# Attention of a two-layer diffusion backbone: the order of four engines written down as a pipeline over three items, and results that share a bank with context scores

## The chip, the core and the metric

The kernel runs on one core of a Trainium2 chip. A core has five engines, each with its own stream of instructions: TensorE (PE in the profile; its weight loads stand apart as PEld), VectorE (DVE), ScalarE (ACT), GpSimd (POOL) and SyncE (SP), which issues transfers. An engine works through its stream in order and waits at an instruction until the semaphores of what it needs have come. Matrix products go to PSUM, eight banks of 512 fp32 values in each of 128 partitions. The metric is the device time of one execution in microseconds, as the median of several runs. Before the change it is 2926.64 us, the median of three (2921.7 to 2929.64).

## What is computed

Two layers over 1024 latent tokens (a grid of 16 rows and 64 columns) and 256 context tokens, width 1024. Layer 0 mixes by Fourier and Hyena groups, layer 1 by neighbourhood attention with 16 heads of 64, and each layer ends with a SwiGLU block. The change concerns the attention of layer 1 only:

```python
s_loc = jnp.einsum("bcqhd,bicjhd->bhcqij", q_r, k_b).astype(jnp.float32) * scale + bias[None]
s_loc = jnp.where(col_ok[:, :, None, :], s_loc, -jnp.inf)
s_ctx = jnp.einsum("bcqhd,bjhd->bhcqj", q_r, kc).astype(jnp.float32) * scale
s = jnp.concatenate([s_loc.reshape(...), s_ctx], axis=-1)
p = jax.nn.softmax(s, axis=-1).astype(v.dtype)
o = (einsum("bhcqij,bicjhd->bcqhd", p_loc, v_b) + einsum("bhcqj,bjhd->bcqhd", p_ctx, vc))
```

Every latent query sees a window of 8 rows by 16 columns, with a bias for the relative position, and all 256 context keys. `y_lat` is the result times `w_out`. Inputs and outputs are float32.

## The kernel before, in words

The program is written with a tile framework. It names tiles in pools (`tile_pool`, with a number of buffers), and the framework finds the dependencies, sets the semaphores and, from a simulated timeline, chooses the order of each engine's instructions. What is traced earlier has the better claim, but an instruction may be moved ahead of another. `issue_after` (`follow`) and `add_manual_dep` add edges by hand.

Precision comes from split operands: a factor is kept as a high and a low half (fp16, or fp32r for queries and keys), and a product is three matmuls (high by high, high by low, low by high).

The attention is cut into 64 *items*. A pair `pr` of heads (0 to 7) has two halves `hf` of the rows, and each half four column chunks `c`. An item holds 128 queries of two heads; for each head it needs 384 local keys (12 rows by 32 columns) and 256 context keys.

- `attn_prep` (L1895) is a generator that projects keys, context keys and queries of one pair, 40 groups of three matmuls into the two `pq` banks, and evacuates each product with ScalarE (high) and VectorE (low): L1951 to L1955 and L1964 to L1966. Between them `value` (L1916) loads a block of values (five per pair) and at once converts it to halves (L1933, L1934). The weights come through `halves_of` on SyncE's queue.
- `attn_item` (L2006) is a generator in three stages. First two bias loads on GpSimd's queue (L2012, tiles of pool `pg`, four buffers) and twelve score matmuls (L2023), context and local for two heads, into four `ps` banks, chained by `follow`. Then the softmax: VectorE takes the minimum over the context (L2033; signs are turned) and adds bias and minimum over the local scores (L2034), ScalarE takes the exponentials (L2036 context, L2038 local). The probabilities are turned by TensorE (L2055: 3 transposes a head, copied to halves at L2058 and L2059). The context part of the first 52 items is split by ScalarE and GpSimd (L2046, L2047) and turned by a DMA on SyncE's queue (L2048); that of the last 12 is turned by TensorE as a third block. Last 30 small matmuls with the values (L2076 to L2078) into one more `ps` bank, and VectorE's reciprocal and multiply (L2080, L2081). The `banks` edges (L2039) hold the next item's scores behind this item's reads.
- `attn_out` (L2087) runs once in four items: four transposes, two copies, a store to memory through GpSimd's queue.
- `attention` (L1980) prepares pair 0 and then goes over the items; between the stages it advances the next pair's preparation to a share of the way, 24 parts for a pair and eight items. After pair 7 a *filler* takes its place, `first_part(0)` (L2344): 6 of 8 blocks of the output projection for the first half of the rows, with weights loaded on GpSimd's queue (L2348), the sum added by VectorE (`add_h`, L2334). Its first column block counts each load of attention output as work. What is left of it runs after the items, then `last_part` (L2368).

PSUM is two pools for the whole program: `pp` with six banks (tiles `ps`) and `pq` with two. During the attention `PS()` goes round the six (L1983). The pools `p4`, `p2`, `pg`, `pt` and `pk` in SBUF hold 20, 34, 4, 6 and 4 tiles.

## Time and profile before

| | |
|---|---|
| median of three runs | 2926.64 us (2921.7 to 2929.64) |
| the profiled execution | 2919.06 us |
| its span, first to last instruction | 2917.3 us |
| granted TensorE clock, mean | 0.979 |
| busy: PE, DVE, ACT, POOL | 2766.0, 2066.4, 1621.9, 609.2 us |
| waits on GpSimd's queue for the transposes that free a bias tile, 1800 to 2235 us | 95.5 us in 57 |

The profile is one execution, recorded by the hardware, in microseconds from the span's start. A line of the timeline gives start, duration, engine, source line, operation, what is written and read, a count, and in brackets the idle time of the engine before it and what ended that. A line of groups gives count, busy time, mean in ns of one, then idle time before the group and its releasers. A line of waits reads: engine and line, what it waited for, total, times, longest. Many matmuls carry L283, the line of the helper, so they are told apart by tiles: `ps<-s,s` with 64 rows are scores, with 128 rows and 65 columns values; `pq<-s,wh` are projections. L274 is the helper for GpSimd's transfers, L268 that for SyncE's.

### The profile page before, as it was taken

Reading aid. Unit: us, or ns where it says so; the run is one execution under the profiler, and the core shown is the slowest. Engines: PE = TensorE matmul, PEld = TensorE weight load, DVE = VectorE, ACT = ScalarE, POOL = GpSimd, SP = SyncE. Lnnn points to the kernel's source line nnn. Section 1 sums busy time; section 2 is a strip of 40 time slices with the busy share of each in tenths; the row PEclk is TensorE's granted clock in tenths of the full one; section 3 lists DMA queues with packets and bytes.
Section 4 is the critical chain, followed back from the end, with each engine's and each line's share of the span. In section 5 each row is a group of like instructions: output and inputs, shape, how many; then the busy total and the mean of one; then the engine's idle time right before and its main releaser. Section 6 shows DMA issues by size and latency. Waiting matters only on the chain. (4 is left out here: it accounts for less than half of the span.)

```text
span 2917.3 us, 46351 instructions
## 1 busy us (share of the span) xinstructions
PE 2766.0 (95%) x16419; PEld 1693.1 (58%) x16419; DVE 2066.4 (71%) x3857; ACT 1621.9 (56%) x2859; POOL 609.2 (21%) x993
## 2 busy tenths in 40 slices
PE   6989999899989999999999999999989999999998
PEld 3755557888879644444555844666665444444555
DVE  5778777585457898877886766666666688765755
ACT  4674325454665676654564555656654476654543
POOL 1012013354121121212120012333333022112000
PEclk8999999999999999999999999999999999999999
DMA  7574435358695665656994897666665666424753
GB/s 264 185 272 170 153 114 173 110 171 303 249 355 176 204 222 190 208 198 254 329 325 152 295 334 270 156 150 160 156 173 186 218 248 224 156 98 176 243 195 116
DMA packets 322083, 607.60 MB, mean 208 GB/s; under 512 B 89910, under 2 KB 129528, under 8 KB 321850
## 3 DMA queue, kind: packets, MB, share of 16 engines
q1 hardware_dynamic: 252378, 384.38, 40.8%
q0 software_dynamic: 67168, 216.06, 20.4%
q10 hardware_dynamic: 2304, 4.20, 0.4%
q8 instruction: 129, 2.11, 0.3%
q14 instruction: 104, 0.85, 0.1%
HBM read 455.33 MB, written 135.53 MB: 203 GB/s over the span
## 5 line engine op out<-in xcount | busy, mean ns | idle before, releaser
L1449 PE MATMUL ps<-s,s 128*128 128x512 f16 x2064 | 467.2, 381 | 10.9 <-ACT g L1454 5.2
L1449 PEld LDWEIGHTS <-s 128*128 128x128 f16 x2640 | 258.0, 98 | 326.0 <-issue 17.8
L283 PE MATMUL ps<-s,wh 128*128 128x256 f32 (+3 forms) x1752 | 398.4, 331 | 11.2 <-ACT wh L287 5.4
L1218 ACT ACTIVATE s<-s,c 128x512 f16<-128x512 f32 (+1 forms) x324 | 232.7, 752 | 134.5 <-DMA s<-d 75.2
L1666 PE MATMUL ps<-s 128*128 128x512 f16 (+2 forms) x1308 | 303.4, 378 | 2.0 <-DVE s L1219 2.0
L1219 DVE SCALAR_TENSOR_TENSOR s<-s,c,s 128x512 f16<-128x512 f32 (+1 forms) x324 | 247.2, 793 | 77.2 <-ACT s L1218 76.2
L283 PE MATMUL pq<-s,wh 128*128 128x512 f16 (+1 forms) x1000 | 276.5, 354 | 9.5 <-DMA wh<-d 2.6
L283 PE MATMUL ps<-s,wl 128*128 128x256 f32 (+3 forms) x876 | 261.9, 331 | 1.1 <-DVE wl L289 0.9
L283 PEld LDWEIGHTS <-wh 128*128 128x128 f16 x1664 | 161.5, 99 | 172.1 <-issue 21.9
L1666 PEld LDWEIGHTS <-s 128*128 128x128 f16 x1536 | 148.5, 98 | 178.9 <-issue 7.0
L274 POOL DMA_DIRECT2D d<-s x201 | 109.1, 543 | 638.7 <-DVE s L1219 160.2
L283 PE MATMUL ps<-s,s 128*128 128x65 f16 (+5 forms) x2922 | 204.8, 244 | 29.0 <-ACT t L2036 14.1
L1449 PE MATMUL ps<-s,wh 128*128 128x512 f16 x616 | 185.8, 380 | 4.9 <-ACT wh L1218 3.4
L335 ACT CAST mat<-cs 128x1024 fp32r<-128x1024 f16 (+2 forms) x120 | 111.4, 934 | 140.1 <-PE ps L283 57.3
L283 PEld LDWEIGHTS ps<-s,wh 128*128 128x128 f32 x1088 | 178.2, 193 | 18.2 <-ACT wh L287 5.7
L283 PE MATMUL ps<-s,mat 128*128 128x512 f32 x696 | 180.5, 405 | 4.7 <-DVE s L289 4.3
L283 PE MATMUL pq<-s,wl 128*128 128x512 f16 (+1 forms) x500 | 173.7, 353 | 0.0
L283 PEld LDWEIGHTS <-s 128*128 128x128 f16 x2400 | 114.5, 98 | 73.9 <-issue 14.9
L283 PEld LDWEIGHTS ps<-s,mat 128*128 128x128 f32 x696 | 133.3, 194 | 38.8 <-DVE s L289 5.6
L1251 ACT ACTIVATE t<-s 128x1024 bf16<-128x1024 f32 (+1 forms) x164 | 141.6, 864 | 15.0 <-DVE c L470 8.6
L1449 PE MATMUL pq<-s,s 128*128 128x512 f16 x576 | 132.6, 380 | 0.7 <-ACT s L1218 0.6
L283 PEld LDWEIGHTS <-wl 128*128 128x128 f16 x832 | 82.0, 99 | 77.9 <-issue 2.6
(434 smaller groups left out, 5476.3 us busy)
## 6 DMA issues: line engine op xcount, KB each, us to landing
s<-d SPq DMA_DIRECT2D x294, 256.0 KB, 4.3
d<-s POOLq DMA_DIRECT2D x157, 256.0 KB, 3.6
s<-in_down SPq DMA_DIRECT2D x154, 256.0 KB, 4.9
s<-in_ada_w POOLq DMA_DIRECT2D x48, 512.0 KB, 5.1
g<-in_bias POOLq DMA_DIRECT2D x128, 192.0 KB, 3.1
s<-in_gate SPq DMA_DIRECT2D x46, 512.0 KB, 3.8
s<-in_up SPq DMA_DIRECT2D x46, 512.0 KB, 4.0
d<-g POOLq DMA_DIRECT2D x87, 256.0 KB, 3.2
```

Of the source, the lines that this page charges most:

```text
L274: self.last_ldr = self.nc.gpsimd.dma_start(out, in_).ins
L283: return self.nc.tensor.matmul(o, l, r, start=st, stop=sp).ins
L335: self.nc.scalar.copy(m, st)
L1218: nc.scalar.activation(hi, src, AF.Copy, scale=scale)
L1219: nc.vector.scalar_tensor_tensor(lo, src, scale, hi, op0=MUL, op1=SUB)
L1251: self.nc.scalar.activation(junk[:, :t.shape[1]], t, AF.Abs, scale=2.0 ** -15, accum_out=st[:, k:k + 1])
L1449: nc.tensor.matmul(ps, x[:, sl], y, start=first and j == 0 and x is wh and y is xh, stop=j == 3 and x is wl, skip_group_check=True)
L1666: m = nc.tensor.matmul(acc[j][:, c0:c1], x[:, sl], y[:, xs], start=first and k == 0, stop=last and k == 2, skip_group_check=True)
```

## The change

The four stages are no longer generators whose order is left to the scheduler. Inside `attention` the order of TensorE, ScalarE, VectorE and GpSimd is taken as written (`manual_schedule`); SyncE's stays with the scheduler. Step `k` of the loop works on three items: bias loads of item k+3, the output of item k-2 if it closes a half, the third turn of item k-1 if it has one, scores and softmax of item k+1, a third of the preparation, the turning transposes of item k, a third, the values of item k-1, the copies of item k's transposes, a third.

PSUM is divided anew for the attention (`accumulators`): two banks `pq` for projections, four `sc` for scores, two `tr` for transposes; the old pools are closed before and opened again after. The result of item k-1 has no bank of its own: it goes to the upper half of the bank that holds the first head's context scores of item k+1. The second head's bias moves from pool `pg` to pool `p2`. A block of values is loaded 11 or so projection groups before it is converted (`loads` and `turns`), and the weights of queries and of the next keys are loaded a little earlier. The hand-made edges go. The matmuls, transposes, exponentials and conversions, their shapes and numbers stay the same. The core of the diff:

```diff
@@ Builder.__init__
-        self.pp = ent(tc.tile_pool(name="pp", bufs=6, space=bass.MemoryType.PSUM))
-        self.pq = ent(tc.tile_pool(name="pq", bufs=2, space=bass.MemoryType.PSUM))
+        self.psum = ent(ExitStack())
+        self.accumulators(pp=6, pq=2)
...
+    def accumulators(self, **banks):
+
+        self.psum.close()
+        for name, n in banks.items():
+            pool = self.tc.tile_pool(name=name, bufs=n, space=bass.MemoryType.PSUM)
+            setattr(self, name, self.psum.enter_context(pool))
...
+    def SC(self):
+        return self.sc.tile([P, 512], F32, tag="sc", name=self.nm("sc"))
+    def TR(self):
+        return self.tr.tile([P, 512], F32, tag="tr", name=self.nm("tr"))
@@ attn_prep
+        qs, vt, staged = {}, [], {}
+        loads, turns = (1, 5, 10, 16, 22), (12, 16, 22, 28, 33)
+        step = 0
+
+        def lin(wh, wl, pc, view=lambda x: x):
+            nonlocal step, acc
+            yield None
+            acc = self.SC() if pr == 0 else self.PQ()
             for kb in range(KB):
                 for w, part in ((wh, 0), (wh, 1), (wl, 0)):
-                    self.mm(acc[pc][:, :WID[pc]], w[:, kb * P:(kb + 1) * P], view(u.ap(part, kb, pc)),
+                    self.mm(acc[:, :WID[pc]], w[:, kb * P:(kb + 1) * P], view(u.ap(part, kb, pc)),
                             kb == 0 and w is wh and part == 0, kb == KB - 1 and w is wl)
+                step += 1
+                for c in range(5):
+                    if step == loads[c]:
+                        load(c)
+                    if step == turns[c]:
+                        value(c)
                 yield WID[pc] / 1024
 
...
+        def load(c):
+            st = staged[c] = self.T()
             if c < 4:
...
+        def value(c):
+            st = staged.pop(c)
+            w = 512 if c < 4 else 256
...
+        acc = None
+        wk = self.halves_of("wk", 0) if pr == 0 else self.aw
         for pc in (0, 1, 2):
...
+            if pc == 1:
+                wq = self.halves_of("wq", pr)
+            yield from lin(*wk, pc)
...
+            if pc == 1 and pr < 7:
+                self.aw = self.halves_of("wk", pr + 1)
+            yield from lin(*wq, pc, by_chunk)
@@ attention
     def attention(self, u, fill):
-        self.prep = {}
+        self.prep, self.osb, self.aw = {}, {}, None
         self.od = [[self.DR([P, LAT], F16) for _ in range(2)] for _ in range(8)]
-        self.banks = 6
-        n = sum(self.attn_prep(0, u))
+        self.accumulators(pq=2, sc=4, tr=2)
+        n = sum(x or 0 for x in self.attn_prep(0, u))
         prep = (x for pr in range(1, 9) for x in (self.attn_prep(pr, u) if pr < 8 else fill))
-        load = (x for pr in range(8) for x in self.attn_load(pr))
-        items, done, self.scores = [], 0, []
-        ahead = 1
-        for k in range(64 + ahead):
-            it = next(load, None)
-            if it is not None:
-                items.append(it)
-            for stage in range(3):
-                i = k - ahead - stage
-                if 0 <= i < 64:
-                    next(items[i], None)
-                while done < (k * 3 + stage + 5) * n / 24:
-                    done += next(prep)
-        for it in items[-2:]:
-            for _ in it:
-                pass
-        self.banks = 8
+        items = [(pr, hf, c) for pr in range(8) for hf in (0, 1) for c in range(4)]
+        state = [{} for _ in items]
+        done = 0
+
+        def piece(step, k):
+            if 0 <= k < 64:
+                step(state[k], *items[k])
+
+        def fetch(target):
+            nonlocal done
+            while done < target:
+                done += next(prep) or 0
+
+        for k in range(2):
+            piece(self.attn_bias, k)
+        e = mybir.EngineType
+        with self.tc.manual_schedule(engines={e.PE, e.Activation, e.DVE, e.Pool}):
+            for k in range(-1, 65):
+                piece(self.attn_bias, k + 3)
+                piece(self.attn_send, k - 2)
+                piece(self.attn_late, k - 1)
+                piece(self.attn_scores, k + 1)
+                fetch((k * 3 + 8) * n / 24)
+                piece(self.attn_turn, k)
+                fetch((k * 3 + 9) * n / 24)
+                free = state[k + 1]["free"] if k + 1 < 64 else self.SC()[:, 256:]
+                if 0 <= k - 1 < 64:
+                    self.attn_values(state[k - 1], *items[k - 1], free)
+                piece(self.attn_turned, k)
+                fetch((k * 3 + 10) * n / 24)
+            piece(self.attn_send, 63)
         for _ in prep:
+        self.accumulators(pp=6, pq=2)
+
+    def attn_bias(self, s, pr, hf, c):
...
+        for hd in (0, 1):
+            b = (self.S2 if hd else self.G)(F32, 384)
+            self.ldr(b, self.a["bias"][pr * 2 + hd, hf, c])
...
+    def attn_scores(self, s, pr, hf, c):
...
+        loc, pctx = ([self.SC(), self.SC()] for _ in range(2))
...
-                    with self.follow(last):
-                        last = self.mm(acc[hd][:, :w], qc[x][r], keys[y][r], x == 0 and y == 0, x == 1)
-                    first = first or last
+                    self.mm(acc[hd][:, :w], qc[x][r], keys[y][r], x == 0 and y == 0, x == 1)
...
-        for r in reads if self.scores[-1] is not own else ():
-            self.tc.add_manual_dep(self.scores[-1], r.ins.name, mybir.DependencyInfo(
-                mybir.DependencyClass.Sync, mybir.DependencyReason.DATA), reason="banks")
...
+        s["pts"], s["free"] = [None] * 3, pctx[0][:, 256:]
+        s["ways"] = [(1, bias[0], 3), (2, bias[1], 3)]
...
+            s["ways"].insert(1, (0, pc, 4))
+
+    def attn_turn(self, s, *item):
+
+        s["ps"] = []
+        for k, src, n in s["ways"][:2]:
+            ps = self.TR()
             for j in range(n):
-                nc.tensor.transpose(ps[:, j * P:(j + 1) * P], src[:, j * P:(j + 1) * P], self.ident)
+                self.nc.tensor.transpose(ps[:, j * P:(j + 1) * P], src[:, j * P:(j + 1) * P], self.ident)
+            s["ps"].append((k, ps, n * P))
+        del s["ways"][:2]
+
+    def attn_turned(self, s, *item):
+
+        for k, ps, w in s["ps"]:
+            t = s["pts"][k] = self.S2(F16, 1024)
+            self.nc.scalar.copy(t[:, :w], ps[:, :w])
+            self.nc.vector.tensor_tensor(t[:, 512:512 + w], ps[:, :w], t[:, :w], SUB)
+
+    def attn_late(self, s, *item):
+
+        if s["ways"]:
+            self.attn_turn(s)
+            self.attn_turned(s)
+
+    def attn_values(self, s, pr, hf, c, o):
...
-        if c == 3:
-            self.attn_out(pr, hf, osb[hf])
-        yield
...
+    def attn_send(self, s, pr, hf, c):
+
+        if c < 3:
+            return
...
+        ps = self.TR()
@@ run, first_part
+                if pc == 0:
+                    yield None
```

In a step, `attn_scores` writes the twelve matmuls and then, for each head in turn, the minimum, the bias step and the two exponentials, so that the reads of one bank follow one another; `attn_values` writes the 30 matmuls, the reciprocal and the multiply.

More of the change, by code (lines that the diff above doesn't have):

```diff
@@ L1936, in value @@
             vt.append((v, lo))
-        if pr == 0:
-            self.aw = self.halves_of("wk", 0)
-        acc = {}
-        wk = self.aw
+        acc = None
+        wk = self.halves_of("wk", 0) if pr == 0 else self.aw
         for pc in (0, 1, 2):
-            for i, s in enumerate(lin(*wk, pc, acc)):
-                if i == 3:
-                    value(len(vt))
-                if pc == 1 and i == 6:
-                    wq = self.halves_of("wq", pr)
-                yield s
+            if pc == 1:
+                wq = self.halves_of("wq", pr)
+            yield from lin(*wk, pc)
@@ L1957, in attn_prep @@
+                nc.vector.scalar_tensor_tensor(kc[:, w:], acc[:, :w], -1.0, kc[:, :w].bitcast(F32), op0=MUL, op1=SUB)
         for pc in (0, 1):
-            for i, s in enumerate(lin(*wq, pc, acc, by_chunk)):
-                if i == 3:
-                    value(len(vt))
-                if pc == 1 and i == 3 and pr < 7:
-                    nxt = self.halves_of("wk", pr + 1)
-                yield s
+            if pc == 1 and pr < 7:
+                self.aw = self.halves_of("wk", pr + 1)
+            yield from lin(*wq, pc, by_chunk)
@@ L2003, in attention @@
         for _ in prep:
             pass
-    def attn_item(self, pr, hf, c, qs, kk, kc, vt, osb):
-        nc, a = self.nc, self.a
-        bias = []
+        self.accumulators(pp=6, pq=2)
+    def attn_bias(self, s, pr, hf, c):
+        s["bias"] = []
         for hd in (0, 1):
-            b = self.G(F32, 384)
-            self.ldr(b, a["bias"][pr * 2 + hd, hf, c])
-            bias.append(b)
-        loc, pctx = ([self.PS(), self.PS()] for _ in range(2))
-        first = last = None
-        qc = [t[:, c * P:(c + 1) * P] for t in qs]
+            b = (self.S2 if hd else self.G)(F32, 384)
+            self.ldr(b, self.a["bias"][pr * 2 + hd, hf, c])
+            s["bias"].append(b)
@@ L2017, in attn_item @@
+    def attn_scores(self, s, pr, hf, c):
+        nc = self.nc
+        qs, kk, kc, _ = self.prep[pr]
+        bias = s["bias"]
+        loc, pctx = ([self.SC(), self.SC()] for _ in range(2))
+        qc = [t[:, c * P:(c + 1) * P] for t in qs[hf]]
         kw = [t.rearrange("p (r w) -> p r w", w=64)[:, 4 * hf:4 * hf + 12, KSTART[c]:KSTART[c] + 32] for t in kk]
@@ L2048, in attn_item @@
             nc.sync.dma_start_transpose(t.rearrange("p (j q) -> p j q", q=P), lies)
[L2049 to L2071 removed]
+            s["pts"][0] = t
+        else:
+            s["ways"].insert(1, (0, pc, 4))
[3 more added lines that the diff above has]
+            ps = self.TR()
+            for j in range(n):
+                self.nc.tensor.transpose(ps[:, j * P:(j + 1) * P], src[:, j * P:(j + 1) * P], self.ident)
[11 more added lines that the diff above has]
+    def attn_values(self, s, pr, hf, c, o):
+        nc = self.nc
+        vt, pts, rv = self.prep[pr][3], s["pts"], s["rv"]
+        if c == 0:
+            self.osb[hf] = self.S2()
+        for i in (0, 1):
+            ops = [(pts[1 + i], g, c, 2 * (hf + g) + i) for g in range(3)]
+            ops += [(pts[0], 2 * i + j, 4, 2 * j + i) for j in range(2)]
             oo = o[:, i * 65:(i + 1) * 65]
```

75 lines of the change are left out of this document (16 added, 59 removed).

## The prediction

> **What bounds the kernel now.** I read the page's head first, then the busy times by stretch, cut at the attention.
>
> ```profile
> span 2917.3 us, 46351 instructions
> PE 2766.0 (95%) x16419; PEld 1693.1 (58%) x16419; DVE 2066.4 (71%) x3857; ACT 1621.9 (56%) x2859; POOL 609.2 (21%) x993
> ```
>
> ```profile
> core 0: us, PE busy (x) PEld busy (x) DVE busy (x) ACT busy (x) POOL busy (x), PEclk, DMA share, GB/s
> 1798.40:1813.90 15.50, 14.94 (x87) 7.73 (x86) 6.12 (x14) 7.13 (x13) 1.17 (x1) 1.00 0.21 61
> 1813.90:2148.10 334.20, 311.60 (x3254) 210.07 (x3253) 209.96 (x586) 203.17 (x432) 127.54 (x200) 0.98 0.65 163
> 2148.10:2246.50 98.40, 92.38 (x898) 57.96 (x896) 65.34 (x165) 47.72 (x101) 32.60 (x62) 1.00 0.52 156
> ```
>
> TensorE is the bound of the whole, and no instruction of it is removed, so all that can be won is time in which it stands or crawls. The three stretches are the attention after the first pair's projections: the lead-in, 51 item steps (from the first use of the 52 DMA-turned items to the last, 6.55 us a step), and the last items with the filler and the last part of the output projection. In the middle stretch 22.6 us are idle and the granted clock is 0.98, another 6.7 us (2% of 334.2).
>
> Next the waits of TensorE in the middle stretch, and one of them in order of time:
>
> ```profile
> PE ps L283 <- ACT t L2036: 10.8, 5, 3.9
> PE ps L283 <- DVE st L2034: 5.3, 7, 1.2
> ```
>
> ```profile
> 1931.52 1.09 POOL L274 DMA_DIRECT2D g<-in_bias  x2 [0.49 <-PE ps L2055]
> 1931.58 1.06 PE L283 MATMUL ps<-s,s 128*128 128x65 f16 x30
> 1931.90 0.47 ACT L2036 ACTIVATE t<-ps,st 128x256 f32<-128x256 f32 x1 [2.12 <-DVE st L2034]
> 1932.28 0.60 ACT L2038 ACTIVATE g<-g,st 128x384 f32<-128x384 f32 x1
> 1932.78 0.85 ACT L2058 CAST s<-ps 128x384 f16<-128x384 f32 x2
> 1935.39 0.62 DVE L2034 CUSTOM_DVE_ANT_0 g<-ps,g,st 128x384 f32<-128x384 f32 x1 [3.87 <-DMA g<-in_bias]
> 1936.05 0.47 ACT L2036 ACTIVATE t<-ps,st 128x256 f32<-128x256 f32 x1 [1.83 <-DVE st L2034]
> 1936.58 1.26 PE L283 MATMUL ps<-s,s 64*128 64x256 f32 x12 [3.94 <-ACT t L2036]
> 1939.11 1.06 PE L283 MATMUL pq<-s,wh 128*128 128x512 f16 x2
> ```
>
> This is the loss in one chain: the bias load is issued only when a turn on TensorE frees one of four bias tiles, lands late, VectorE waits 3.87 us for it, the exp (L2036) follows, and the next item's scores, tied by hand to these reads, stand 3.94 us; after it two projections take 1.06 us. What they take undisturbed, and the rest of a step, shows in a clean stretch:
>
> ```profile
> 1883.39 1.15 PE L283 MATMUL ps<-s,s 64*128 64x256 f32 x12 [1.71 <-ACT t L2036]
> 1884.48 0.87 PE L2055 MATMUL ps<-c,g 128*128 128x128 f32 x6
> 1885.19 0.59 PE L283 MATMUL pq<-s,wh 128*128 128x512 f16 x2
> 1885.62 0.38 PE L283 MATMUL pq<-s,wl 128*128 128x512 f16 x1
> 1893.17 1.07 PE L283 MATMUL ps<-s,s 128*128 128x65 f16 x30
> 1894.08 0.52 PE L2091 MATMUL ps<-c,s 128*128 128x128 f32 x3
> 1906.29 0.38 PE L283 MATMUL pq<-s,wh 128*128 128x256 f16 x2
> 1906.51 0.27 PE L283 MATMUL pq<-s,wl 128*128 128x256 f16 x1
> ```
>
> From start to next start: scores 1.09, turn 0.71, values 0.91 us; a 512-wide projection 0.215 (0.43 for two), a 256-wide one 0.11. The disturbed pair's 1.06 against 0.59 is the halved clock.
>
> **What the 51 steps need.** The counts of projections in the middle stretch (two with wh to one with wl):
>
> ```profile
> L283 PE MATMUL pq<-s,wh 128*128 128x512 f16 x417 | 126.3, 382 | 2.7 <-DVE s L1954 1.9 <-DVE s L1966 0.8
> L283 PE MATMUL pq<-s,wh 128*128 128x256 f16 x103 | 17.3, 272 | 0.4 <-DVE s L289 0.3
> ```
>
> 625 x 0.216 + 155 x 0.11 = 152.0; 51 x (1.09 + 0.71 + 0.91) = 138.2; 12 output transposes at about 0.45 (four at the turn's pace) 5.4. Together 295.6 of 334.2: 38.6 us are lost, the 22.6 idle, the 6.7 of clock and some 9 of slow starts. That is the most the middle stretch can give.
>
> **Part by part.** *Bias loads.* They are issued three steps ahead (half of the tiles come from another pool), while a step is 5.7 us or more and the load above, issued at 1931.52, was used at 1935.39, at most 3.9 us later. I cost this wait at nothing; the cover is two whole steps. *The hand-made tie* between scores and the reads before them goes; in its place come four score banks, all taken by each item.
>
> *The written order.* One step is scores (k+1), a third of the projections, turn (k), a third, values (k-1), a third. Per pair the projections are 96 x 0.216 + 24 x 0.11 = 23.4 us for eight steps, 0.97 a third. So TensorE's plan from the first score is: scores to 1.09, turn 2.06 to 2.77, values 3.74 to 4.65, end 5.62, with 0.45 more in two steps of eight. What must keep up:
>
> ```profile
> 2117.48 1.15 PE L283 MATMUL ps<-s,s 64*128 64x256 f32 x12
> 2118.13 0.76 DVE L2033 TENSOR_REDUCE st<-ps 128x1 f32<-128x256 f32 x2 [1.32 <-PE ps L283]
> L2046 ACT CAST s<-t 128x512 f16<-128x512 f32 x51 | 31.9, 625 | 0.0
> L2080 DVE RECIPROCAL st<-ps 128x2 f32<-128x2 f32 x50 | 8.2, 164 | 21.5 <-PE ps L283 21.5
> L2081 DVE TENSOR_TENSOR s<-ps,st 128x128 f32<-128x128 f32 x50 | 14.4, 289 | 1.3
> L2059 DVE TENSOR_TENSOR s<-ps,s 128x384 f16<-128x384 f32 x102 | 55.3, 552 | 43.2 <-ACT s L2058 40.4 <-issue 2.1 <-POOL s L1932 0.5
> L1933 ACT ACTIVATE s<-t,c 128x512 f16<-128x512 f32 (+1 forms) x31 | 21.4, 690 | 18.1 <-DMA t<-d 13.4 <-PE ps L283 4.7
> L1934 DVE SCALAR_TENSOR_TENSOR s<-t,c,s 128x512 f16<-128x512 f32 (+1 forms) x32 | 23.5, 735 | 18.5 <-ACT s L1933 18.2
> ```
>
> VectorE's reduction starts 0.65 us after the first score matmul (2117.48, 2118.13). Its bias step needs the local scores, so starts at about 1.2; with 0.62 and its read-out it is done at 1.9. Four exps spaced as above (0.38 and 0.50) take 1.76, the low-half copy 0.62: ScalarE is free at 4.3. The values end at about 4.8, reciprocal and multiply (0.16 + 0.29) at 5.3. These two read the result out of the bank that the next scores write at 5.62: 0.3 us to spare. That is a clean step. In five of eight steps an evacuation of the projections, or a value block, stands ahead of the reciprocal (by the program's counts: key splits, the last query split and the first value block fall in the first two thirds; four value blocks and the first query split in the last). On such a step ScalarE works to 5.0, VectorE to 5.7, the multiply ends near 6.1 and the scores wait about 0.4. In two of eight the output transposes want a transpose bank that is free only after its copy (0.43, half of the two at 1932.78) and subtraction (0.55) behind the multiply, near 5.85 or later: about 0.4 each. Sum 5 x 0.4 + 2 x 0.4 = 2.8 us in eight steps, 0.35 a step, 17.9 in 51. Bounds: 0, if the overlap of neighbouring instructions (rows start 0.38 after one of 0.47) gives the 0.3 to 0.5 back; 34, twice as much, if each late step hands its backlog on (after a value block in the last third VectorE is busy to 6.9 while its next reduction is due at 5.62 + 0.65). I take the middle, since three steps of eight carry nothing extra and let the backlog run out. Middle stretch: 295.6 + 17.9 = 313.5, or -20.7 us.
>
> The clock is one place where a rule helps. The rows show a 3.94 us gap followed by halved matmuls, and the stretch's 0.98. The Trainium skill, TensorE: Matmul & The Clock Gate, Part 1, says that an idle window of about 3.4 us halves the clock and another busy one restores it. By that rule, with which the trace agrees, waits of 0.4 us leave the clock whole and the 6.7 us come back entirely; a new wait above 3.4 would cost some 1.7 more than itself.
>
> *GpSimd's queue.* Its order is written down too. Of its work the value memsets and low halves keep their engine and have slack (127.54 busy of 334.2). But the filler's weights (wh, wl of the output projection) are loads on that queue, written directly ahead of the matmuls that use them.
>
> ```profile
> 2152.07 0.54 POOL L274 DMA_DIRECT2D wh<-d  x1 [2.88 <-PE pq L283]
> wl<-d POOLq DMA_DIRECT2D x8, 192.0 KB, 3.3
> s<-s SPq DMA_TRANSPOSE x52, 3.6
> ```
>
> Before, the scheduler could set other matmuls into that gap. Now, where such a load falls in a step with an output store (by the counts steps 57 and 61), GpSimd waits for the store's subtraction until about 1.9 us (an estimate: the transposes' 0.45, then a copy and a subtraction of 512 columns at some 0.7 each, from the 384-wide 0.43 and 0.55), issues three DMAs (3.5), and the weights land at 6.8 while TensorE asks at 3.7: 3 us each, 6 in all (0 to 8). In four steps the filler counts loads as work and TensorE has only 4.2 us to do (1.09 + 0.71 + 0.91, a third turn and a share of the output transposes 0.55, one and a half groups of three projections 0.97). There the third turn, at the head of the next step, closes a ring: reduction to exps 1.25, exps 1.76, two copies 0.86, subtraction 0.55, third turn 0.45, its copy and subtraction 1.3, next reduction: about 6.1, so 4 x 1.9 = 7 us (0 to 10). Against these 13 stand 6.0 us of idle in that stretch (98.40 less 92.38) and, at the middle stretch's rate (9 of 334; the clock is whole here), 2.7 of slow starts. Net +4.3, bounds -9 to +14.
>
> *The ends.* The PSUM pools are closed and opened again. At the start:
>
> ```profile
> 1774.95 0.60 PE L283 MATMUL pq<-s,wh 128*128 128x512 f16 x2 [2.63 <-DMA wh<-d]
> 1778.98 1.06 ACT L1880 COPY t<-ps 128x512 f32<-128x512 f32 x2
> ```
>
> Projections started at 1774.95 while the old banks were read until 1780.04. If the new pools wait for all of these, 5.1 us; if only bank by bank, nothing. With the same question at the end, I take +2 (0 to 7). The lead-in of 15.5 us stays.
>
> **Sum.** -20.7 + 4.3 + 2 = -14.4. The profiled execution (2919.06 us, 1.8 outside the span) would become 2904.7. It lies 7.6 below the median of the runs shown, 2926.64; against that the forecast is 2912.
>
> **Rivals.** *All waits hidden*: the 17.9 vanish, about 2894. For it: VectorE and ScalarE are busy for 209.96 and 203.17 of 334.2 us, which leaves room by the averages. Against: they alternate, and must answer each other three times a step. *Nothing left*: backlog is handed on, 34 us of waits, -4.6 + 4.3 + 2 = +1.7, 2928; the scheduler's order, which could fill each gap with projections, then lost no more than a fixed one. *Slower*: the shared bank and the strict order make VectorE and ScalarE the bound. The place is the reciprocal behind an evacuation; it decides once the mean wait passes 0.63 us a step (38.6 less 6.3, over 51), and at 1 us a step the sum is 51 - 38.6 + 6.3 = +18.7, 2945. For it: VectorE is already late by 0.6 after each value block in the last third. A second lock would come with it: if the values may not write the bank before the other item's first exp has read it, at 2.4 us in a clean step, a backlog of 1.4 reaches their 3.74. The Trainium skill, PSUM — Partial Sum Buffer, PSUM bank collisions, asks for such guarding by bank rather than by address; no run here shows it yet, and the price is within the 1 us. *Not what it says*: SyncE is not in the written order, so its transposes and value loads may fall late; with 3.6 us to land (the median above) against two steps this needs a blocked queue, and I put it with the slower case.
>
> **Chances.** Forecast 0.45 (own range 2899 to 2921), all hidden 0.17, nothing left 0.21, slower 0.17. About 0.3% (8.8 us) is what a measurement of this kernel can tell from no change. Faster by more: 0.40 of the forecast's and 0.17, 0.57; same 0.21 + 0.05, 0.26; slower 0.17. The range 2892 to 2938 leaves out most of the slower case and the fast edge, some 0.2.
>
> **What would show it.** Right: no bias wait on VectorE, no TensorE gap over 3.4 us in the steps, clock 1.00, steps of 6.1 us, and scores waiting on the multiply by a few tenths. Wrong: TensorE waiting for the evacuations or weights by several us, steps of 6.5 or more, or a hole at the pools' change.

## The result and the profile after

| | before | after |
|---|---|---|
| median | 2925.03 us (2915.02 to 2935.09, seven runs beside those of after) | 2946.6 us (2943.7 to 2954.41, seven runs) |
| ratio, 95% interval | | 1.0081 (1.0059 to 1.0103) |
| profiled execution, its span | 2919.06, 2917.3 us | 2943.7, 2941.8 us |

The change makes the kernel slower by some 21 to 24 us (17 to 30 by the interval). That is the rival with the other sign, and 2946.6 lies above the range. The head of the page after, then the stretches, cut at the same places as before (first score, first and last DMA transpose, and an end that gives the three stretches as many matmuls in sum, 4238 to before's 4239):

```profile
span 2941.8 us, 46325 instructions
PE 2765.3 (94%) x16419; PEld 1689.4 (57%) x16419; DVE 2078.4 (71%) x3857; ACT 1622.9 (55%) x2857; POOL 602.8 (20%) x993
```

```profile
core 0: us, PE busy (x) PEld busy (x) DVE busy (x) ACT busy (x) POOL busy (x), PEclk, DMA share, GB/s
1802.40:1809.50 7.10, 6.10 (x34) 3.06 (x34) 2.67 (x7) 4.43 (x7) 1.22 (x2) 1.00 0.50 150
1809.50:2151.60 342.10, 312.00 (x3261) 205.54 (x3258) 219.57 (x585) 206.50 (x436) 119.97 (x200) 1.00 0.66 150
2151.60:2266.60 115.00, 102.76 (x943) 63.62 (x944) 71.65 (x171) 50.53 (x103) 34.93 (x68) 0.96 0.51 162
```

TensorE's work is the same. The 51 steps, meant to shrink, grow from 334.2 to 342.1 us, though the clock there is whole (1.00 rounded; one stretch of 3.4 us at half is shown below) and no wait for a bias load is left, both as forecast. Lead-in and last stretch together go from 113.9 to 122.1. TensorE's waits in the 51 steps, engine and line, what it waited for, total, times, longest:

```profile
PE tr L2119 <- DVE s L2082: 15.1, 12, 1.7
PE sc L296 <- DVE s L2108: 10.0, 13, 1.0
PE sc L296 <- ACT t L2053: 4.2, 7, 0.8
```

In order: the output transposes wait for a transpose bank (the turned copies' subtraction frees it); the scores wait for the multiply that reads the result out of the shared bank; the values wait for the exp that reads the other columns of that bank. One such step, all engines in order of time:

```profile
1970.34 1.01 DVE L2082 TENSOR_TENSOR s<-tr,s 128x384 f16<-128x384 f32 x2
1971.27 0.41 DVE L2050 TENSOR_REDUCE st<-sc 128x1 f32<-128x256 f32 x1
...
1971.82 0.62 DVE L2051 CUSTOM_DVE_ANT_0 g<-sc,g,st 128x384 f32<-128x384 f32 x1
...
1972.53 0.48 ACT L2053 ACTIVATE t<-sc,st 128x256 f32<-128x256 f32 x1 [2.48 <-DVE st L2051]
...
1974.04 0.60 ACT L2055 ACTIVATE s<-s,st 128x384 f32<-128x384 f32 x1
1974.54 0.61 ACT L2060 CAST s<-t 128x512 f16<-128x512 f32 x1
...
1975.05 0.72 ACT L1956 ACTIVATE s<-t,c 128x512 f16<-128x512 f32 x1
...
1975.68 0.84 ACT L2081 CAST s<-tr 128x384 f16<-128x384 f32 x2
1975.81 1.12 DVE L1957 SCALAR_TENSOR_TENSOR s<-t,c,s 128x512 f16<-128x512 f32 x1 [2.18 <-ACT s L1956]
1975.87 0.38 PE L296 MATMUL pq<-s,wl 128*128 128x512 f16 x1
...
1976.86 0.16 DVE L2107 RECIPROCAL st<-sc 128x2 f32<-128x2 f32 x1
1977.05 0.29 DVE L2108 TENSOR_TENSOR s<-sc,st 128x128 f32<-128x128 f32 x1
1977.26 1.01 DVE L2082 TENSOR_TENSOR s<-tr,s 128x384 f16<-128x384 f32 x2
...
1977.95 0.63 PE L2119 MATMUL tr<-c,s 128*128 128x128 f32 x4 [1.70 <-DVE s L2082]
```

Follow it from one subtraction (1970.34) to the next (1977.26): the reductions come behind the subtractions, ScalarE stands 2.48 us until VectorE has the bias step, then does four exps, the low-half copy, a value block and two turned copies almost without a pause (0.16), while VectorE stands 2.18; then VectorE's half of the value block, reciprocal, multiply, subtractions. Between the two subtractions VectorE and ScalarE stand at the same time for 0.14 us at most; they hand one piece of work to each other. The way round, called the ring from here on, takes 6.92 us, against the 5.8 (295.6 / 51) that TensorE needs for a mean step; what TensorE loses by it here is the 1.70 at the end. In eight steps that repeat through the attention, the way round by the starts of these subtractions is 5.13, 6.69, 6.91, 7.9, 6.5, 5.79, 6.29 and 8.07, in sum 53.3; 5.13 is a step with no evacuation in the ring. The sum must be TensorE's period, since the pattern repeats, so it shows no cause by itself; 7.9 and 8.07 are the steps in which the output's copy and subtraction stand in the ring and wait for TensorE's transposes. Whether the ring sets the pace is for the experiments.

The rows of waits count idle time alone. The wait for the multiply stands between the seventh and the eighth of the twelve score matmuls:

```profile
2010.34 0.80 PE L296 MATMUL sc<-s,s 64*128 64x256 f32 x7
2012.03 0.77 PE L296 MATMUL sc<-s,s 64*128 64x384 f32 x5 [0.89 <-DVE s L2108]
```

By the starts of these two matmuls, which fall together in an undisturbed step, it is 0.38 to 1.31 us in 23 of 50 steps, 18.5 us in sum; the row of L2108 above has 10.0 of it.

And one wait cost more than itself. From 1.5 us behind the end of this step's 1.70 the granted clock (the value after POOL's) is halved:

```profile
1979.40:1982.80 3.40, 3.40 (x19) 2.55 (x16) 2.44 (x7) 1.64 (x4) 0.55 (x1) 0.50 0.68 207
```

Three transposes take 0.84 us there and 0.49 elsewhere, and the step from these scores to the next is 6.98 us long where the same step of the pattern is otherwise 5.38. Five more waits of 1.70 to 1.72 in these steps had no such effect.

The change of the pools, TensorE's rows, and the two stretches there:

```profile
1768.66 0.38 PE L296 MATMUL ps<-wh,s 128*128 128x512 f16 x1
1776.82 1.01 PE L296 MATMUL sc<-s,wh 128*128 128x512 f16 x2 [7.77 <-ACT t L1893]
```

```profile
1769.10:1776.80 7.70, 0.00 (x0) 0.10 (x1) 7.70 (x13) 5.64 (x11) 2.00 (x4) 0.63 1.03 402
1776.80:1802.40 25.60, 25.59 (x120) 12.16 (x119) 8.80 (x19) 5.09 (x9) 3.82 (x12) 0.91 0.53 185
```

The new pools wait for the last reader of the old banks (the copy at L1893): a hole of 7.77 us where there were 2.63, and then projections at half pace (1.01 for two, 0.59 elsewhere), so that pair 0 takes 25.7 us to its first score instead of 23.7.

The difference of the two spans, 24.5 us, by starts of rows: the hole 5.1 and the slow projections 2.0; first score to first product of the SwiGLU block, 489.8 before and 506.1 after, 16.4; behind it 4.3 (628.9 and 633.2); ahead of the hole -3.3. The last two lie where only the placement of other work could differ: behind it the seventeen kernels below, with the same code there, take 631 to 640 us, so these two are not explained.

### The profile page after: what moved, and what is told of

Same layout as the page of the kernel before. It is cut to its first block, busy times and chain, and to the rows that moved or that the text cites. A ratio compares the mean times of both kernels' runs of the same rounds, so it can differ in the third digit from the quotient of the medians.

```text
span 2941.8 us, 46325 instructions
## 1 busy us (share of the span) xinstructions
PE 2765.3 (94%) x16419; PEld 1689.4 (57%) x16419; DVE 2078.4 (71%) x3857; ACT 1622.9 (55%) x2857; POOL 602.8 (20%) x993
## 5 line engine op out<-in xcount | busy, mean ns | idle before, releaser
L1462 PE MATMUL ps<-s,s 128*128 128x512 f16 x2244 | 506.3, 381 | 10.2 <-ACT g L1467 6.0
L296 PE MATMUL pq<-s,wh 128*128 128x512 f16 (+1 forms) x908 | 252.1, 354 | 5.9 <-DMA wh<-d 4.0
L296 PEld LDWEIGHTS <-wh 128*128 128x128 f16 x1664 | 153.6, 99 | 163.0 <-issue 33.7
L296 PE MATMUL sc<-s,s 128*128 128x65 f16 (+3 forms) x2688 | 154.7, 234 | 16.5 <-DVE s L2108 10.0
L296 PE MATMUL pq<-s,wl 128*128 128x512 f16 (+1 forms) x454 | 157.9, 354 | 0.0
L2053 ACT ACTIVATE t<-sc,st 128x256 f32<-128x256 f32 x128 | 60.7, 474 | 144.3 <-DVE st L2051 138.5
```

The costliest lines, as they stand in the source:

```text
L296: return self.nc.tensor.matmul(o, l, r, start=st, stop=sp).ins
L1462: nc.tensor.matmul(ps, x[:, sl], y, start=first and j == 0 and x is wh and y is xh, stop=j == 3 and x is wl, skip_group_check=True)
L2053: nc.scalar.activation(pc[:, i * 256:i * 256 + 256], pctx[i][:, :256], AF.Exp, bias=mx[:, i:i + 1], scale=-1.0)
```

## The experiments

Ratios are to the kernel before, with 95% interval, beside after's 1.0081; "attention" is the time from the first score to the first product of the next block in the one profiled execution (before 489.8, after 506.1 us). A stretch of halved clock as the one above costs it some 1.6 us; the 51 steps of the runs hold 0 to 3 of them, and more in the three runs without the whole written order. Rows of waits are from 1815 to 2160 us. "The steps" is the time from the second item's first score matmul to the 53rd's (before 331.7, after 338.5).

### The places where TensorE waits

**Output transposes behind the scores.**

```diff
-                piece(self.attn_send, k - 2)
                 piece(self.attn_late, k - 1)
                 piece(self.attn_scores, k + 1)
+                piece(self.attn_send, k - 2)
+                piece(self.attn_softmax, k + 1)
+                piece(self.attn_store, k - 2)
```

`attn_scores` keeps the matmuls, `attn_softmax` has the rest of it; `attn_store` is the subtraction and the store out of `attn_send`.

> The output transposes of the half just done go behind the score matmuls of the item two ahead, their copy ahead of that item's exps on ScalarE and their subtraction behind its bias steps on VectorE; nothing else moves. In the changed kernel they stand at the head of a step, 2.1 and 1.2 us late in every eight steps, since the transpose bank that they take is free only after the last subtraction of the step before. Theory A, that this bank's wait is a loss of its own: some 2.9 of the 53.3 us of eight steps go, 12 to 19 us in all, a time near 2931 and a ratio to the kernel before of 1.001 to 1.005. Rival B, that VectorE and ScalarE are the bound by their ring of answers and the place of the wait is chance: the same time is waited at the scores instead, less than 4 us go, and the ratio stays at 1.007 to 1.010.

1.008 (1.0059 to 1.0100), attention 506.3: nothing gained. Its waits:

```profile
PE tr L2083 <- DVE tk L2139: 19.3, 12, 2.0
PE sc L296 <- DVE s L2118: 4.1, 7, 1.0
```

Now the turns wait, for the bank that the output holds until its own subtraction. B's number came, but not quite by B's way: the steps are shorter (333.8), and the last eleven items take back as much (84.6 us after 79.6). That the bank has three users was not yet excluded.

**Output transposes in a third bank.** In `attn_send`, `ps = self.PQ()` for `ps = self.TR()`.

> The output transposes stay where the changed kernel has them, at the head of a step, but take a bank of the projections' pair (of which one at a time is being summed) instead of one of the two transpose banks, which the turns of every step need. Theory A, that three users of two transpose banks in the steps with an output are the largest loss: the twelve waits of 1.2 to 2.1 us in the 51 steps fall under 0.3 each, and 12 to 18 us go: near 2931, ratio 1.001 to 1.004. Rival B, the ring of VectorE and ScalarE: the same time comes back at the scores and values in those steps, less than 5 us go, ratio 1.006 to 1.010.

1.0049 (1.0032 to 1.0065), attention 496.5: between the two.

```profile
PE sc L296 <- DVE s L2108: 7.9, 12, 1.0
PE pq L2119 <- DVE s L2108: 5.0, 6, 0.8
PE pq L296 <- DVE tk L2122: 4.6, 6, 0.8
PE sc L296 <- ACT t L2053: 4.1, 7, 0.8
```

The 15.1 for the transpose bank are gone; 9.6 came back, half of it because the transposes now stand right behind the multiply that makes their data, half because the next projection waits for the bank they took.

**Values sooner.**

```diff
                 piece(self.attn_turn, k)
-                fetch((k * 3 + 9) * n / 24)
                 ...
                     self.attn_values(...)
+                fetch((k * 3 + 9) * n / 24)
                 piece(self.attn_turned, k)
```

> The value products of the item behind go ahead of the second third of the projections instead of behind it, so that reciprocal and multiply come ahead of the evacuation that this third ends with, and the shared bank is read out about a microsecond sooner. Theory A, the prediction's slower case at its place (the reciprocal behind an evacuation): the waits of the scores for the multiply, 2.6 us in eight steps, go, the evacuation is then behind the multiply and the turned copies a little later, so the output transposes wait as before or 0.5 longer: 8 to 16 us less, near 2935, ratio 1.002 to 1.006. Rival B, that the two engines' work of a step is simply too long for it: what the scores gain, the transposes lose, within 4 us of the changed kernel, ratio 1.007 to 1.010.

1.0039 (1.0023 to 1.0055), attention 496.2: inside A's range, and the mechanism is half of A's.

```profile
PE sc L296 <- ACT t L2053: 15.9, 29, 1.8
PE tr L2119 <- DVE s L2082: 10.0, 11, 1.8
```

The wait for the multiply is gone, as A has it; the outputs' wait fell from 15.1 to 10.0 and the values' wait for the exp went from 4.2 to 15.9, which A does not have.

**Both.**

> The output transposes in a bank of the projections' pair, and the values ahead of the whole second third of the projections. With the values sooner alone the scores no longer waited for the multiply, but the values waited 15.9 us in all for the exp that reads their bank, and the transposes 10.0. Theory A, separate losses: the 10 us of the transposes go from that run as well, near 2932, ratio 0.999 to 1.003, better than the third bank alone by 3 to 6. Rival B: no better than the values sooner alone, ratio 1.004 or more.

1.0045 (1.0027 to 1.0063): no better than the values alone, B's number, although the attention in the profiled execution is shorter (489.3); that execution is the fastest of the eight, 2931.36 us beside a median of 2938.12.

**The result in the other head's bank.** `s["free"] = pctx[1][:, 256:]` for `pctx[0]`.

> One word of the changed kernel: the result goes into the free half of head 1's context-score bank instead of head 0's. Head 1's exp reads its bank about 1.1 us after head 0's, so if the values may not write a bank before the exp that reads its other half is done, they now wait in most steps with extra work on ScalarE; and the bank is head 1's context bank again in the next scores, half a microsecond sooner than the local bank that head 0's becomes. Theory A, that sharing a bank is a cost of its own: the values' wait for the exp, 4.2 us in the 51 steps, grows to 15 to 40, the time by 8 to 30 us, ratio 1.011 to 1.018. Rival B, that the values would stand behind VectorE and ScalarE in any bank: within 4 us of the changed kernel, ratio 1.007 to 1.010.

1.0107 (1.0084 to 1.0130), attention 509.9: between the two.

```profile
PE sc L296 <- ACT t L2053: 22.9, 32, 1.8
PE tr L2119 <- DVE s L2082: 8.4, 6, 1.4
PE sc L296 <- DVE s L2108: 0.4, 1, 0.4
```

The lock is real: the values, which write columns 256 to 385, wait for the exp that reads columns 0 to 255, and 4.2 us become 22.9. The program guards by bank, as the Trainium skill asks in PSUM — Partial Sum Buffer, PSUM bank collisions; what an unguarded access would do no run here shows. But the other two waits give nearly all of it back, 29.3 in sum before and 31.7 now. In this pair the place decides where TensorE waits, hardly how long.

**The pools later.** `self.accumulators(pq=2, sc=4, tr=2)` behind pair 0's `attn_prep`, which takes `PQ()`.

> The pools are closed and opened behind the first pair's projections instead of ahead of them; these run in the old two banks, as in the kernel before. Theory A, that the new pools wait for the last readers of all old banks: the 7.8 us hole ahead of the projections shrinks to the 2.6 us of the kernel before and their clock is whole again, 4 to 7 us less, near 2941, ratio 1.005 to 1.007. Rival B, that the hole only moves to the pools' new place (first scores behind the query split): 0 to 2 us less, ratio 1.007 to 1.009.

1.005 (1.0036 to 1.0065). TensorE at that place:

```profile
1778.44 0.38 PE L296 MATMUL ps<-wh,s 128*128 128x512 f16 x1
1781.81 1.03 PE L296 MATMUL pq<-s,wh 128*128 128x512 f16 x2 [2.98 <-DMA wh<-d]
```

A: the hole is back to 2.98, as before waiting for a weight, and it does not turn up at the first scores (the first item's step is 8.3 us long instead of 9.8). The half pace stays, which A does not have: 1.03 for two projections.

**Third bank, values half a third sooner (`fetch((k * 3 + 8.5) * n / 24)` ahead of them), pools later.**

> Three edits at once: the output transposes in a bank of the projections' pair, the values halfway into the second third of the projections (so that the result is read about half a microsecond sooner, and the values still come behind the exp whose bank they share), and the pools changed behind the first pair's projections. Theory A, that the three losses are separate: 12 to 18, 5 to 10 and 5 us, together some 25, near 2921, ratio 0.996 to 1.001. Rival B, that VectorE and ScalarE are the bound: at most 12 together, ratio over 1.003.

1.0012 (1.0000 to 1.0024), attention 490.8: between A and B. Three places mended together give back 0.7 per cent, 20 us, the pools' share included.

**The same, outputs two steps later** (`piece(self.attn_send, k - 4)`).

> The three edits of the earlier run (output transposes in a bank of the projections' pair, values half a third sooner, pools changed behind the first pair's projections), and the output transposes two steps later. In the earlier run they stood at the step's head right behind the multiply whose result they turn (5.0 us of waits in the 51 steps), and the next projection then waited 4.6 us for the bank that they had taken. By the program's counts the projections change their bank in the second, third and fourth step after the end of a half, not in the third step's first part, where the transposes now stand. Theory A, that each wait is a matter of place: these 9.6 us go, 2 come back in VectorE's and ScalarE's backlog, the time from the first scores to the next phase falls from 491 to 483 to 486, and the ratio to 0.996 to 0.9995. Rival B, that VectorE and ScalarE have no room left: less than 3 us, ratio 1.000 to 1.002.

1.0037 (1.0023 to 1.0051), attention 497.1, worse than without it and outside both ranges. The expected 9.6 us did go from the outputs, and as much came back:

```profile
PE sc L296 <- ACT t L2054: 14.1, 28, 1.5
PE sc L296 <- DVE s L2109: 9.8, 19, 0.7
```

(L2109 is this kernel's multiply, whose waits were 1.6 in the run before; L2054 is the exp, there 12.1.) The steps are level, 330.9 after 331.1, so A, that each wait is a matter of place, fell here. What makes the run worse stands behind the steps: from the last item's first score matmul to the next block 83.9 us after 78.4, for which the cause was not traced.

### The order

**No written order**, `with nullcontext():` for `manual_schedule`; then the same with the score matmuls chained by `follow` as before.

> The same pieces, pools and shared bank, but no written order: the scheduler is free again on all engines. Theory A, that the fixed order loses the time since nothing may fill a gap: the items come back to 6.3 us a step or less, and with the hole at the pools' change still there the time is 2915 to 2932, ratio 0.997 to 1.002. Rival B, that the division of the banks (two for transposes, four for scores, the result shared) is the cause whatever the order: 2940 or more, ratio over 1.005, with TensorE waiting for the same banks.

> No written order, as in the earlier run with a free scheduler, but the twelve score matmuls of an item are chained again in the order of the program, as the kernel before had them. In the free run the scores of an item took 1.7 us instead of 0.9, since matmuls of the two heads were no longer neighbours. Theory A, that this is what made the free run 50 us longer than the changed kernel: back to 2925 to 2945. Rival B, that with banks divided into two, four and two the scheduler's order is bad by itself: still above 2960.

1.0234 (1.0210 to 1.0257) and 1.0355 (1.0334 to 1.0377). B both times: with the banks divided into two, four and two and the result shared, the scheduler is 45 to 80 us worse than the written order. The chain of the scores was not the reason, and which wait is was not settled. Part of it is the clock: from 1815 to 2150 us 0.96 and 0.94 were granted, 0.99 in after, by which some 10 and 17 us of that stretch go (an estimate, 0.03 and 0.05 of 335).

**TensorE's order alone**, `engines={e.PE}`.

> The written order holds for TensorE alone; ScalarE, VectorE and GpSimd are put in order by the scheduler again. Theory A, that TensorE's fixed order against banks is what costs and the other engines' order is right as written: within 6 us of the changed kernel or slower, ratio 1.006 to 1.012. Rival B, that the written order of VectorE and ScalarE (an evacuation ahead of a reciprocal or of an exp) is what makes the waits: the scheduler puts the urgent ones first, 8 to 20 us less, ratio 1.001 to 1.005.

1.0136 (1.0116 to 1.0157), attention 517.2: slower than A's range, and against B. With TensorE's order as written, the written order of the other engines is worth 11 us in the attention against the scheduler's. The clock has its part here too (0.96 granted from 1815 to 2150 us).

### The length of the ring

Three edits that touch no bank. The low-half copy stands in the ring (1974.54 above): all of ScalarE's work behind it, and the subtractions that need that, come 0.6 us later for it.

**Behind the turned copies**: the copy (L2060), GpSimd's subtraction and the DMA transpose are made a piece of their own.

```diff
                 piece(self.attn_turned, k)
+                piece(self.attn_lies, k + 1)
```

> The low-half copy of the context probabilities (0.605 us on ScalarE, in the first 52 items), with GpSimd's subtraction and the DMA transpose behind it, is issued behind the turned copies of the item before instead of ahead of them; the work is the same. Theory R, the ring: reductions and bias step 1.12, exps 2.16, low-half copy 0.61, turned copies 0.86, last subtraction 0.55, next reductions, some 5.3 us and with the evacuations that stand in it 6 to 7; it gets 0.6 us shorter in each step that it binds: 10 to 25 us less than the changed kernel, 2922 to 2937, ratio 0.999 to 1.004, and all three waits of TensorE shrink together. Rival P, the places (banks): VectorE and ScalarE do as much as before, the waits stay at their banks, within 4 us of the changed kernel.

1.0029 (1.0014 to 1.0044), attention 489.1, 17.0 less.

```profile
PE sc L296 <- ACT t L2054: 7.9, 15, 0.8
PE tr L2127 <- DVE s L2090: 5.7, 13, 0.7
PE sc L296 <- DVE s L2116: 3.8, 13, 0.5
```

No engine does less, and the waits fall from 29.3 to 17.4 in sum. R's sign that all three shrink did not come: the outputs' and the multiply's do (15.1 and 10.0 before), the values' wait for the exp grows from 4.2 to 7.9.

**On GpSimd**: `nc.gpsimd.tensor_copy(lies[:, :512], pc)` for `nc.scalar.copy`.

> The same copy made by GpSimd, which is busy for 115 us of these 334 and has only the subtraction behind it. Theory R: as with the copy behind, and a little more, since ScalarE has 0.6 us less in every step: 12 to 28 us less, 2919 to 2935, as long as the DMA-turned probabilities still come in time for the values a step and a half later (copy and subtraction on GpSimd some 2.3 us, then 3.6). Rival P: within 4 us of the changed kernel, or slower if the DMA transposes come late.

1.0007 (0.9992 to 1.0022), attention 482.8, 23.3 less.

**Twice on ScalarE**, the first time as `nc.scalar.copy(lies[:, 512:], pc)`.

> The same copy made twice on ScalarE, the first into the half that GpSimd overwrites afterwards; the result is the same. ScalarE goes from 61 to 70 per cent busy in the items, far from full by the average. Theory R: the ring gets 0.6 us longer in each of 52 steps, and nearly all of it is lost, 20 to 31 us more than the changed kernel, 2967 to 2978, ratio 1.0145 to 1.019. Rival P: an engine that is 70 per cent busy has room, less than 8 us more, ratio under 1.011.

1.0171 (1.0146 to 1.0195), attention 531.3, 25.2 more. A copy row is 0.605 us long, but ScalarE's next row starts 0.51 behind its start (1974.54 and 1975.05 above), which makes 26 us in 52 copies; of the 25.2 some 3 are clock (10.2 us of the steps at half pace, 3.4 in after). So most of the added length, not all, is lost, on an engine that is free for a third of the time. The waits with the copy twice, then with it on GpSimd:

```profile
PE sc L296 <- DVE s L2109: 20.8, 21, 1.5
PE tr L2120 <- DVE s L2083: 18.9, 11, 2.2
PE sc L296 <- ACT t L2053: 7.3, 7, 1.1
```

```profile
PE tr L2119 <- DVE s L2082: 9.6, 13, 1.3
PE sc L296 <- DVE s L2108: 3.6, 13, 0.4
PE tr L2073 <- DVE s L2082: 2.7, 1, 2.7
PE sc L296 <- ACT t L2053: 1.1, 3, 0.7
```

All three come out as theory R has it and outside P's ranges; only the 2979 us of the doubled copy are 1 above R's. Made twice, the copy raises each of the waits of 15.1, 10.0 and 4.2; on GpSimd it lowers each, at the same banks (the 2.7 at L2073 is one wait for a third turn, behind the steps).

**Behind, with third bank, values half a third sooner, pools later.**

> The copy behind the turned copies, together with the three edits of the sixth run (output transposes in a bank of the projections' pair, values half a third sooner, pools changed behind the first projections; 1.0012). Theory R: the waits that are left there, 23 us in the 51 steps, come down by half or more, 10 to 18 us: 2909 to 2920, ratio 0.994 to 0.998, faster than the kernel before. Rival P: the same as the sixth run, 1.000 to 1.0025.

0.9983 (0.9969 to 0.9996), attention 479.8: 11 us less than without the copy's move and faster than the kernel before; a little short of R's ratio, and outside P's.

**On GpSimd, third bank, pools later; then the filler's weights on SyncE's queue too** (`self.ld` for both in `first_part`).

> The low-half copy on GpSimd, the output transposes in a bank of the projections' pair, the pools changed behind the first pair's projections; the values at their old place, since with the copy gone from ScalarE they wait for the shared bank's exp only 1.1 us. Theory R, the ring with what is left at its places: from the copy on GpSimd alone some 7 us less in the items and 5 at the pools, near 2918, ratio 0.995 to 0.999. Rival: the output's copy and subtraction stand in the ring wherever their transposes go, so only the pools' 5 us come, ratio 0.9985 to 1.0005.

> The same, with the filler's weights loaded on SyncE's queue, which is not in the written order, instead of GpSimd's. The prediction's step: 6 us of waits for these weights go (4 are seen), 2 to 6 less than the run beside it, ratio 0.993 to 0.998. Rival: the loads come no sooner, since their two buffers come free only with the matmuls before, within 1.5 us of the run beside it.

0.9984 (0.9974 to 0.9994) and 0.996 (0.9943 to 0.9976), medians 2919.08 and 2911.22 beside 2924.32: the second is the fastest kernel of this study, 13 us under the one before. Attention 478.7 and 472.2; the steps take 314.0 and 314.3 us, 24 less than in after. The rows for the filler's weights, from 2160 to 2290 us, in after and in the first of these two runs; in the second no such row is left:

```profile
PE pq L296 <- DMA wh<-d: 4.0, 2, 2.3
```

```profile
PE pq L296 <- DMA wh<-d: 3.8, 2, 2.0
```

The 3.8 us are part of the 6.5 that the attention got shorter; the rest was not traced.

## Why the prediction was wrong

The failed step is the waits of the 51 steps: "Sum 5 x 0.4 + 2 x 0.4 = 2.8 us in eight steps, 0.35 a step", with 0.67 as the worst. Lost are 342.1 - 295.6 = 46.5 us, 0.91 a step, so the stretch came out at +7.9 instead of -20.7: 28.6 of the 38.9 by which the span missed (+24.5 instead of -14.4). Of the 46.5, 30.1 are TensorE idle; of the other 16.4, 8.5 are waits inside the rows of scores (18.5 less 10.0) and 1.6 the halved clock, and the rest was not traced. The prediction had also put at nothing, without a reason, the 9 us of slow starts that it read in this stretch of the kernel before. The mechanism was named; its size was taken from the wrong sum.

- The clean step was worked out as what each engine owes TensorE: exps and copy until 4.3, multiply at 5.3, "0.3 us to spare". The way back was left out: behind 4.3 stand two turned copies (0.86) and the last subtraction (0.55), and only then the next reductions, which were due at 6.27. For the last items I did close this ring ("about 6.1"); for the steps I did not. From the first reduction at 0.65 that is 0.65 + 5.06, and 5.13 was measured in the step without an evacuation; with 0.7 of an evacuation on ScalarE and 0.75 on VectorE inside it is 6.5, and steps of 6.5 to 6.9 were measured. By the starts of the subtractions it is over TensorE's 5.8 in six of the eight steps listed above and level with it in one. That the ring sets the pace is shown by the three runs on the low-half copy: the same work behind, 17.0 us less; off ScalarE, 23.3 less; twice, 25.2 more.
- "Three steps of eight carry nothing extra and let the backlog run out" fell: the score starts of clean steps are 5.34 us apart, just what their matmuls take, and the ring alone takes 5.13, so such a step works off only some 0.2 of a backlog.
- The outputs' wait, "about 0.4 each", is 15.1 over 12, 1.3 each: the largest single error. The wait for the multiply was 18.5 in 23 of 50 steps, 0.8 each, where I had 0.4 in five of eight.
- The shared bank was thought to be the next scores' first bank. Wherever the trace shows the scores waiting for the multiply, it is at their eighth matmul, the first local product of the second head, which is due some 0.45 us behind the first. This error was on the other side, and the second lock, "a backlog of 1.4 reaches their 3.74", is there with 4.2 us.
- The "slower" rival was right: VectorE and ScalarE "the bound", mean wait past 0.63, 2945 at 1 us a step. That 2946.6 is so near is partly luck: by the rival's own sum the measured 0.91 gives +14.1, 2941, and the rest is the hole and the unexplained 4.3 behind the attention. Its place, the reciprocal behind an evacuation, is one of three. Averages spoke against it (after the change 219.57 and 206.50 busy of 342.10), and averages cannot see a ring. It had 0.17.
- Bias waits and clock came nearly as forecast: no such wait, PEclk 1.00 rounded, no TensorE gap over 1.72 us in the steps. But the clock was halved once behind a wait of 1.70 (above), so the length of a wait alone does not tell whether it costs the clock. The Trainium skill, TensorE: Matmul & The Clock Gate, Part 1, has the clock halved after an idle window of about 3.4 us. The half pace after the hole of 7.77 agrees; half pace after 2.98 (1.03, above) and after 1.70 do not, if the window is read as the length of a wait, and the measurement decides. After 2.63 in before the pace was full (0.60). The kernel before was also halved twice, from 1937.5 for 3.4 us and from 2128.6 for 6.8, the second time behind a wait of 2.27; that is some 5.1 us to win, where the prediction took 6.7 from a rounded 0.98.
- Lead-in and last items: +4.3 forecast for the last, +8.2 measured with the lead-in, inside the bounds (by its own terms, 18 less 8.7, the upper one is +9, not +14); the weights' waits were 4.0 us, two of 2.3 at most, where I had two of 3.
- The ends: +2 (0 to 7) against 5.1 and 2.0 at the start. "If the new pools wait for all of these, 5.1 us" was the right branch; the 2.0 of slow projections behind the hole was in neither.
- *Nothing left* supposed that the scheduler's order lost no more than a fixed one. Free order with these banks costs 45 to 80 us more than the written one, in part by the clock. So with these banks the loss lies in the ring and the shared places, not in writing an order down; a written order with the old banks was not tried.

## What to carry to other kernels

Where several engines answer each other within one step, write down the way round, from one instruction to the same instruction of the next step, with every queue-mate in between, and compare it with the bound engine's step; busy shares of 60 and 64 per cent say nothing on it. If waits move to another place when one is taken away, do not only mend places (three of them together gave back 20 us here): make the ring shorter too (one copy moved gave 15 to 22) by moving an instruction that nobody needs at once behind those that somebody waits for, or to an engine outside the ring. Doubling one instruction that stands in the suspected ring, with the result unchanged, tells in one run whether it is one, if the clock is looked at as well.

## What was not expected of the hardware

GpSimd made the low-half copy (128x512, fp32 to fp16) in rows as long as ScalarE's, 0.616 us to 0.605:

```profile
L2060 POOL CAST s<-t 128x512 f16<-128x512 f32 x51 | 31.4, 616 | 134.1 <-ACT t L2053 134.1
```

The Trainium skill, Perfetto Trace Analysis, Optimizing GPSIMD Operations, advises to prefer other engines, GpSimd being generally slower. By the start of the next row it is slower here too (from 1970.31 to 1971.00 in that run, 0.69 us, where ScalarE had 0.51), yet the move was worth 0.74 per cent: the copy left the ring for an engine that had room.
